# Moving the sums of the down-projection's weights into the first up-projection, the operand groups of x a step later, and the first pair's weights into other pages

## The chip, the cores and the metric

The kernel runs on one core of a Trainium2 chip. The metric is the device time of one execution in microseconds (us); several runs are made and their median is taken. The core's engines run side by side, each through its own list of instructions: TensorE (PE in the profile) multiplies matrices, VectorE (DVE) and ScalarE (ACT) work element by element, GpSimd (POOL) and SyncE (SP) do little here but issue transfers. Transfers between the main memory (HBM) and the on-chip memory (SBUF) are carried by 16 DMA engines that all issuers share. Matmul results stand in PSUM, from where DVE or ACT takes them.

## The reference, cut to what matters

One layer of a decoder on x of 2048 positions by 1024 channels:

```python
h = rms_norm(x, norm1_g)
lru_x, lru_gate, sc_b, sc_c, sc_x = jnp.split(h @ w_in, splits, axis=-1)   # 1024 -> 2*1024 + 3*512
lru_x = causal_dwconv(lru_x, lru_conv_w) + lru_conv_b                      # 4 taps
y_lru = rg_lru(lru_x, ...) * gelu(lru_gate)          # gates by 16 blocks of 64x64, then a scan along time
y_sc = sc_b * causal_dwconv(sc_c * sc_x, sc_conv_w)                        # 3 taps
x = x + concatenate([y_lru, y_sc]) @ w_out                                 # 1536 -> 1024
h = rms_norm(x, norm2_g)
gate, up = jnp.split(causal_dwconv(h @ w_up, ffn_conv_w), 2, axis=-1)      # 1024 -> 2*3072, 3 taps
x = x + (gelu(gate) * up) @ w_down                                         # 3072 -> 1024
return rms_norm(x, final_g)
```

All of it is float32. The four matrix products w_in, w_out, w_up and w_down are nearly all of the arithmetic.

## The kernel before, in words

**Float32 by three matmuls.** `split` (L228, L229) makes of each operand a high part (ACT, a copy to the rounded type) and a low part (DVE, a subtraction). Each product of a 128x128 block of weights with 512 positions is then three matmuls: high by high, high by low, low by high. So ACT and DVE have a split to do for each weight and each operand, and TensorE waits for both parts.

**Fewer products.** Most block products of two by two are made with seven products instead of eight (Strassen's scheme in Winograd's form). They need sums and differences of blocks: of the weights, called S1 to S4 beside the plain blocks W11, W12, W22, W21, and of the operands, called T1 to T4 beside B11, B21, B22. `TERMS` lists the seven products as pairs of such names. The sums of the weights of w_in are made on DVE in the first stage and kept in HBM (`si_d`). Those of w_down are made by transfers alone, in HBM (`sd_d`): `sums` (L941 and on) writes a list `pieces` of 24 pieces of 512 KB, six each for S1, S3, S2, S4. `sum_step` (L400 to L407) takes the next piece: it issues a copy of one block on SP (L404), and with a lag of two steps a transfer on Pool that adds the other block to a copy made earlier (L407, an accumulate). S2 adds the finished S1, and S4 the finished S2, so some accumulates read what others have written.

**The stages.** The sequence is worked in two halves of 1024 positions:

1. in-projection of half 0 (`in_phase`, 0 to 336 us), with direct products;
2. out-projection of half 0 (`sweeps`, 336 to 458 us): seven sweeps of three steps, each step with 24 matmuls for each of two k (L992). Beside it, `x1_beside` (after steps 2, 6, 11 and 16 of 21) makes the operands of half 1's in-projection: four groups, one for each call of `x1_prep`. A group is two loads, a handful of DVE sums and differences (L607 to L614) and four splits with the names hhB11x, hhB21x, hhT1x, htx and their low parts;
3. in-projection of half 1 (`in_blocks`, 458 to about 790 us): 14 pairs of output blocks, 84 matmuls each (L666). The first pair goes through `spread`, which for each of four k runs all seven products; the others go term by term. Beside the pairs run the convolutions, the gates (L369, L380) and the scans. `beside_blocks(j)` is called once for a pair: `mean0` loads and squares the first half's result for its norm (L1140, L1147), and two calls of `sum_step` follow;
4. out-projection of half 1 (from about 790 us);
5. up-projection of half 0 (`up_phase(0)`, 942 to 1378 us): 24 pairs of 84 matmuls. `up_weights` issues three loads of weights for the pair after the next (L629 to L631), makes S1 to S4 on DVE (L640) and splits them. `UpPair.open` clears the first two columns of two pages with Pool (L329), and `keep_halo` copies the last two columns with Pool (L336);
6. down-projection of half 0 (1378 to 1607 us), the first that reads `sd_d`; then the up- and down-projection of half 1.

**What sets the order.** On TensorE, SP and Pool instructions run as the program writes them. On ACT and DVE a scheduler sets the order by priorities; `high_priority` moves some forward. Each engine's list is worked strictly in turn, so an instruction that waits holds all behind it.

**Pages.** SBUF tiles come from named rings; a tile waits until its page's last reader is done. Raw weights of the sweeps and of `up_weights` are loaded into "wr" (6 pages, `raw_tile`), their split parts stand in pages that `wpage` and `vpage` take by turns from a ring of ten: two "w" and eight "v". `in_weights` (L807 and on, loads at L816) loads two weight blocks of the in-projection at a time into a "w" page; for the first four terms of the first pair (`V0`) the split parts go to "v" pages, for all others to "wr".

Of the kernel before, what the change touches and what calls it, by code (L numbers as in the profile page):

```python
# [28 lines left out]
NR = 6  # L29
LP = 0  # L30
LW = 400
LEAD = 3
HALVES = (slice(0, P // 2), slice(P // 2, P))
HW = 90
# [3 lines left out]
NI = NFF // 2  # L38
# [29 lines left out]
PAIR_OF = {o: (PAIRS.index(p), i) for p, ab in BLOCKS.items() for i, o in enumerate(ab)}  # L68

TERMS = [("W11", "B11"), ("S1", "T1"), ("S2", "T2"), ("S3", "T3"), ("W22", "T4"), ("S4", "B22"), ("W12", "B21")]  # L70
V0 = [w for w, _ in TERMS[:4]]
KEPT = ["W11", "W12", "W22"]
SPILLED = ["S3", "S1", "S2", "S4"]

# [14 lines left out]
def block_kernel(  # L89
# [37 lines left out]
    def blocks(name, ops, n):  # L127
        return {o: [dr.tile([P, 2, NB], F32, name=f"{name}_{o}_{k}") for k in range(n // 2)] for o in ops}
# [4 lines left out]
    sd_d = blocks("sd_d", S_OPS, NI)  # L133
    si_d = [dr.tile([P, 4, NB], F32, name=f"si_d{i}") for i in range(len(PAIRS))]
    x2_d = [[dr.tile([2, P, T], F32, name=f"x2_d{h}_{m}") for m in range(KC // 2)] for h in range(NH)]
# [5 lines left out]
    def page(name, tag, bufs):  # L141
        return sb.tile([P, 2, NB], F32, name=name, tag=tag, bufs=bufs)
# [10 lines left out]
    def wv_page(name, tag):  # L153
        return page(name, tag, NW if tag == "w" else NWV - NW)

    def tmp(name):
        return page(name, "tmp", 7)
# [4 lines left out]
    def raw_tile(name):  # L162
        return page(name, "wr", NR)
# [7 lines left out]
    def flat(t):  # L171
        return t.rearrange("p a b -> p (a b)")
# [54 lines left out]
    def split(hi, lo, src):  # L227
        nc.scalar.activation(r32(hi), src, AF.Copy)  # L228
        nc.vector.tensor_tensor(r32(lo), src, hi, ALU.subtract)  # L229
# [71 lines left out]
    def mean_split(acc, name):  # L301
        n = acc.shape[-1]
        hi = flat(tmp(f"rh_{name}"))[:, :n]
        lo = flat(tmp(f"rl_{name}"))[:, :n]
        with tc.high_priority(offset=HP):
            split(hi, lo, acc)
        return hi, lo
# [93 lines left out]
    def sum_step():  # L401
        if pieces:
            dst, src, add = pieces.pop(0)
            nc.sync.dma_start(dst, src)  # L404
            adds.append((dst, add))
        if len(adds) > 2 or adds and not pieces:
            nc.gpsimd.dma_start(*adds.pop(0), accum_op=ALU.add, max_dma_last_dim=2 * T)  # L407
# [186 lines left out]
    def x1_prep(k, rs, side=0):  # L594
        return operands(f"x_{k}", k, lambda kk: xT[kk, :, T:S], O_G1, rs, side)
# [30 lines left out]
    def up_weights(half, j):  # L626
        n = f"up{half}_{j}"
        ta, tb, tcd = (raw_tile(f"wr{k}_{n}") for k in "abc")
        nc.sync.dma_start(ta[:, 0, :], w_up[j, 0])  # L629
        nc.sync.dma_start(tcd, w_up[j, 2:4].rearrange("h p c -> p h c"))  # L630
        nc.sync.dma_start(tb[:, 0, :], w_up[j, 1])  # L631
        tick()

        def two(src, name):
            hi, lo = wpage(f"wh{name}_{n}"), wpage(f"wl{name}_{n}")
            split(hi, lo, src)
            return [(hi[:, i, :], lo[:, i, :]) for i in range(2)]

        def add(dst, a, b):
            nc.vector.tensor_tensor(dst, a, b, ALU.add)  # L640

        w11, w12, w22, w21 = ta[:, 0, :], tb[:, 0, :], tcd[:, 0, :], tcd[:, 1, :]
        s1, s2, s3, s4 = ta[:, 1, :], tb[:, 1, :], tcd[:, 1, :], ta[:, 1, :]
        add(s1, w22, w21)
        add(s2, s1, w11)
        add(s3, w11, w21)
        p11, p1 = two(ta, "a")
        p12, p2 = two(tb, "b")
        p22, p3 = two(tcd, "c")
        add(s4, s2, w12)  # L650
        d = wpage(f"whd_{n}")
        split(d[:, 0, :], d[:, 1, :], s4)
        return {"W11": p11, "W12": p12, "W22": p22, "S1": p1, "S2": p2, "S3": p3, "S4": (d[:, 0, :], d[:, 1, :])}
# [112 lines left out]
    def up_rest(half, j, ug, un):  # L766
        cg, cu = flat(tmp(f"cg{half}_{j}")), flat(tmp(f"cu{half}_{j}"))
        conv(cu, un, 3, O_FCW + 3 * (NFF + j))
        conv(cg, ug, 3, O_FCW + 3 * j)
        nc.scalar.activation(cg, cg, AF.Gelu_apprx_tanh)  # L770
        nc.vector.scalar_tensor_tensor(cu, cg, -1.0, cu, ALU.mult, ALU.mult)
        when = {NFF - 2: 3, NFF - 1: 6}.get(j, 1)
        if j % 2 == 0:
            combine_even(f_d[half], when, j // 2, cu, cg)
            even.append((cu, cg))
        else:
            a, c = even.pop()
            combine_odd(f_d[half], when, j // 2, a, cu, c, (cg[:, :NB], cg[:, NB:]))

    def up_phase(half, hs, between):  # L780
        wts = [up_weights(half, 0), up_weights(half, 1)]
        cur = UpPair(half, 0, hs, wts[0])
        for j in range(NFF):
            if j + 2 < NFF:
                wts.append(up_weights(half, j + 2))
            nxt = UpPair(half, j + 1, hs, wts[j + 1]) if j + 1 < NFF else None
            if j == 0:
                cur.spread()
                nxt.begin()
                nxt.sum1()  # L790
            elif nxt is None:
                cur.middle(cur.sum1)
                cur.second()
                cur.fourth()
                cur.end()
            else:
                cur.middle(cur.second)
                nxt.begin()
                cur.fourth()
                if j + 2 < NFF:  # L800
                    nxt.sum1()
                cur.end()
            up_rest(half, j, cur.ug, cur.un)
            cur = nxt
            between(j)

    def in_weights(ops):  # L807
        n = "_".join(f"{i}{op}" for i, op in ops)
        raw, m = wv_page(f"wr_in{n}", "w"), len(ops)
        for at, (i, op) in enumerate(ops):  # L810
            if op in KEPT:
                o, h = BLOCKS[PAIRS[i]][op[1] == "2"], slice(0, NB) if op[2] == "1" else slice(NB, T)
                src = w_in[o][:, h]
            else:
                src = si_d[i][:, SPILLED.index(op), :]
            nc.sync.dma_start(raw[:, at, :], src)  # L816
        out = []
        for at, (i, op) in enumerate(ops):
            home = vpage if i == 0 and op in V0 else raw_tile
            t = home(f"w{op}_in{i}")  # L820
            split(t[:, 0, :], t[:, 1, :], raw[:, at, :])
            out.append((t[:, 0, :], t[:, 1, :]))
        return out
# [142 lines left out]
    def sums(src, dst, n):  # L966
        for o, a, b in SUMS:
            for i2 in range(n // 2):
                t = flat(dst[o][i2])
                add = src[W_OPS.index(b), i2] if b in W_OPS else flat(dst[b][i2])  # L970
                pieces.append((t, src[W_OPS.index(a), i2], add))

    def sweeps(half, wsrc, fsrc, ni, name, residual, done, beside, tail=0, lead=0):
# [6 lines left out]
        for s, (wo, fo, on_x) in enumerate(SWEEPS):  # L980
# [20 lines left out]
            for i2 in range(ni // 2):  # L1001
# [5 lines left out]
                parts = []  # L1007
                with tc.high_priority(offset=LW if step < lead else HW):
                    for raw, n in zip(raws, "wf"):
# [32 lines left out]
    def acc_tile(name):  # L1042
        return flat(tmp(f"ss_{name}"))
# [29 lines left out]
    tick()  # L1073
    tick()
    store_queue[0] = nc.sync
    sums(w_down, sd_d, NI)


    def x1_beside(s):
        if s in (2, 6, 11, 16):  # L1080
            hx.append(x1_prep(len(hx), ss1[1]))

    def wsrc(w, sums):
# [19 lines left out]
    def res_alloc(key, n):  # L1103
# [9 lines left out]
        x_residual(0, res_alloc),  # L1113
        store_done(x2_d[0], None, "b0"),
        x1_beside,
    )

    rs2 = [[], []]
# [12 lines left out]
    hs = [[], []]  # L1131
    def squares_then_mean(src, name, out, first):
        acc = acc_tile(name)
        held = []

        def between(n):
            k = n - first
            if 0 <= k < KC:
                t = flat(tmp(f"sx_{name}_{k}"))
                nc.sync.dma_start(t, src(k))  # L1140
                held.append(t)
            if 1 <= k <= KC:
                t = held[k - 1]
                if k == 1:
                    nc.scalar.activation(acc, t, AF.Square)
                else:
                    nc.scalar.activation(t, t, AF.Square)  # L1147
                    nc.vector.tensor_tensor(acc, acc, t, ALU.add)
            if k == KC + 1:
                held.append(mean_split(acc, name))  # L1150
            if k == KC + 2:
                out.append(inv_rms(acc, name, held[-1]))

        return between
# [2 lines left out]

    def beside_blocks(j):
        mean0(j)
        sum_step()  # L1160
        sum_step()

    store_queue[0] = nc.gpsimd
    late_gates = in_blocks(hx, beside_blocks)
    store_queue[0] = nc.sync

# [10 lines left out]
    def out1_beside(s):  # L1177
# [14 lines left out]
        out1_beside,  # L1192
        lead=LEAD,
    )

    up_phase(0, hs[0], squares_then_mean(lambda k: x2_d[1][k // 2][k % 2], "b1", rs2[1], 2))

    ss3 = acc_tile("c0")

# [151 lines left out]
```

## Time and profile before

| what | value |
|---|---|
| median of the runs | 2310.24 us (2309.06 to 2311.68, 3 runs) |
| the profiled execution | 2310.52 us |
| its span in the trace | 2308.7 us, 1.8 less |
| mean granted clock of TensorE | 0.988 |
| data moved by DMA | 415 MB, 180 GB/s in the mean |

The span is what the profiler sees between first and last instruction; the time of the run holds a little more around it. In a page's rows a line is `line engine operation out<-in`, with the count behind an x. A row of a time line gives the start in us, the length in us, and in brackets the engine's idle time before it and what ended it. In the rows of waits stand the total, the number of times and the longest. The granted clock is 1.00 at full speed. "SPq" and "POOLq" are transfers issued by SP and Pool.

### The profile page before, as it was taken

The page shows a single profiled execution, that of the slowest core. Times are in us where ns is not written, and L with a number is a line of the kernel's source. Part 1 is how long each engine was busy: PE and PEld are TensorE (multiplying, and loading weights), DVE is VectorE, ACT ScalarE, POOL GpSimd, SP SyncE. Part 2 cuts the span into 40 slices and gives each one's busy share as a digit, 9 for nine tenths or more (in the row PEclk, how much of TensorE's full clock was granted, in tenths as well). Part 3 has the DMA queues.
Part 4 walks back from the last instruction along what each step waited for, and adds up shares of the span by engine and source line. Part 5 has one row for each costly group of instructions (what it writes and reads, how often), then busy time and mean ns, then how long its engine had stood idle before and what let it go on. Part 6 is the DMA issues. An engine that isn't in the chain of part 4 may idle for free.

```text
span 2308.7 us, 26404 instructions
## 1 busy us (share of the span) xinstructions
PE 2242.5 (97%) x9750; PEld 1825.3 (79%) x9750; DVE 1787.3 (77%) x2070; ACT 1214.7 (53%) x1403; POOL 179.0 (8%) x298
## 2 busy tenths in 40 slices
PE   9999999999889989999999999999999999999997
PEld 7787787777667768888888888888888888888886
DVE  8868878846667799789898877677888888876556
ACT  7648834457577844455555444444554444443343
POOL 0021110000111100001010100000000000100000
PEclk9999999999999989999999999999999999999999
DMA  7575367657777868243332347676223232359754
GB/s 276 162 222 173 120 244 257 235 173 206 203 215 211 257 214 298 96 144 123 119 107 99 110 160 286 204 246 208 87 96 110 96 110 96 110 187 328 252 197 157
DMA packets 157952, 415.00 MB, mean 180 GB/s; under 512 B 16640, under 2 KB 19328, under 8 KB 157248
## 3 DMA queue, kind: packets, MB, share of 16 engines
q1 hardware_dynamic: 136960, 356.96, 45.1%
q0 software_dynamic: 20720, 56.37, 9.2%
q8 instruction: 76, 1.25, 0.2%
q14 instruction: 52, 0.43, 0.1%
q10 hardware_dynamic: 144, 0.00, 0.0%
HBM read 311.55 MB, written 139.46 MB: 195 GB/s over the span
## 4 chain that ended last, share of the span: by engine, by line
PE 65%; issue 2%; ACT 2%; DVE 2%; DMA 1%; POOL 0%; SPq 0%; DVEq 0%; ACTq 0%; POOLq 0%
PE zx L666 22%; PE dx L992 11%; PE zc L666 11%; PE dy L992 8%; PE za L666 5%; PE ox L992 2%; PE oy L992 2%; PE zxin L666 1%; PE zS L666 1%; PE zW L666 1%; PE zcin L666 0%; DMA sx_b<-x_d 0%; DMA wr_in9S_9S<-si_d 0%; DMA sd_d_S<-in_w_down 0%; ACT r L380 0%
## 5 line engine op out<-in xcount | busy, mean ns | idle before, releaser
L229 DVE TENSOR_TENSOR fl_d<-wrf_d,fh_d 128x1024 fp32r<-128x1024 f32 x84 | 102.7, 1223 | 120.3 <-ACT fh_d L228 117.9
L228 ACT ACTIVATE fh_d<-wrf_d 128x1024 fp32r<-128x1024 f32 x84 | 88.9, 1059 | 201.9 <-PE dy L992 78.3
L992 PE MATMUL dx<-fh_d,wh_d 128*128 128x512 f32 x384 | 149.4, 389 | 0.0
L992 PE MATMUL dx<-fl_d,wh_d 128*128 128x512 f32 x384 | 149.4, 389 | 0.0
L992 PE MATMUL dx<-fh_d,wl_d 128*128 128x512 f32 x384 | 149.4, 389 | 0.0
L229 DVE TENSOR_TENSOR wla_up<-wra_up,wha_up 128x1024 fp32r<-128x1024 f32 x48 | 58.8, 1225 | 110.0 <-ACT wha_up L228 110.0
L284 PE MATMUL zin_b<-xh,wl_in 128*128 128x512 f32 x448 | 138.7, 391 | 2.6 <-DVE wl_in L229 2.6
L284 PE MATMUL zin_b<-xh,wh_in 128*128 128x512 f32 x448 | 139.7, 393 | 0.7 <-ACT xh L452 0.4
L284 PE MATMUL zin_b<-xl,wh_in 128*128 128x512 f32 x448 | 138.7, 390 | 0.1
L345 DVE SCALAR_TENSOR_TENSOR cg<-ug,prm,cg 128x1024 f32<-128x1024 f32 x96 | 122.9, 1280 | 8.2 <-ACT cg L341 7.3
L345 DVE SCALAR_TENSOR_TENSOR cu<-un,prm,cu 128x1024 f32<-128x1024 f32 x96 | 122.8, 1279 | 4.7 <-ACT cu L341 4.3
L666 PE MATMUL zc<-hhB,whd_up 128*128 128x512 f32 x368 | 120.8, 389 | 0.0
L666 PE MATMUL zx<-ht,whc_up 128*128 128x512 f32 x368 | 113.3, 389 | 0.0
L992 PE MATMUL dy<-fh_d,wh_d 128*128 128x512 f32 x288 | 112.0, 389 | 0.0
L992 PE MATMUL dy<-fl_d,wh_d 128*128 128x512 f32 x288 | 112.0, 389 | 0.0
L992 PE MATMUL dy<-fh_d,wl_d 128*128 128x512 f32 x288 | 112.0, 389 | 0.0
L677 ACT ACTIVATE ug<-zx 128x512 f32<-128x512 f32 x92 | 54.9, 596 | 103.0 <-PE zx L666 98.1
L229 DVE TENSOR_TENSOR wl_d<-wrw_d,wh_d 128x1024 fp32r<-128x1024 f32 x84 | 102.3, 1219 | 8.3 <-ACT wh_d L228 7.0
L284 PEld LDWEIGHTS zin_b<-xh,wh_in 128*128 128x128 f32 x448 | 83.7, 188 | 24.4 <-DVE yc L557 1.5
L284 PEld LDWEIGHTS zin_b<-xh,wl_in 128*128 128x128 f32 x448 | 84.5, 189 | 20.6 <-DVE wl_in L229 3.0
L228 ACT ACTIVATE fh_o<-wrf_o 128x1024 fp32r<-128x1024 f32 x42 | 44.5, 1059 | 106.5 <-PE ox L992 28.3
L284 PEld LDWEIGHTS zin_b<-xl,wh_in 128*128 128x128 f32 x448 | 84.4, 188 | 18.1 <-DVE xl L453 0.5
(549 smaller groups left out, 6406.1 us busy)
## 6 DMA issues: line engine op xcount, KB each, us to landing
wrc_up<-in_w_up SPq DMA_DIRECT2D x48, 512.0 KB, 4.7
f_d_T<-cg SPq DMA_DIRECT2D x96, 256.0 KB, 2.5
wrw_d<-sd_d_S SPq DMA_DIRECT2D x48, 512.0 KB, 4.9
wrf_d<-f_d_T SPq DMA_DIRECT2D x48, 512.0 KB, 4.1
f_d_B<-cu SPq DMA_DIRECT2D x72, 256.0 KB, 2.4
wrw_d<-in_w_down SPq DMA_DIRECT2D x36, 512.0 KB, 4.8
wrf_d<-f_d_B SPq DMA_DIRECT2D x36, 512.0 KB, 3.4
wr_in<-in_w_in SPq DMA_DIRECT2D x25, 512.0 KB, 7.1
```

Of the source, the lines that this page charges most:

```text
L228: nc.scalar.activation(r32(hi), src, AF.Copy)
L229: nc.vector.tensor_tensor(r32(lo), src, hi, ALU.subtract)
L284: nc.tensor.matmul(ps[t], r32(a), r32(b[:, blk(t)]), start=(first and i == 0), stop=(last and i == 2))
L345: nc.vector.scalar_tensor_tensor(dst, src[:, k : k + T], col(o_w + k), dst, ALU.mult, ALU.add)
L666: nc.tensor.matmul(ps, r32(p[:, s]), r32(self.hs[k][x][o]), start=f and i == 0, stop=l and i == 2, skip_group_check=True,)
L677: nc.scalar.activation(dst, self.x, AF.Copy)
L992: nc.tensor.matmul(ps[m], r32(p), r32(x[:, k, :]), start=first and i == 0 and n == 0, stop=(last or not on_x) and i == ni - 1 and n == 2, ...
```

## The change

Three edits, all of order and place; the arithmetic stays.

1. The list of the w_down sums is written just before `up_phase(0)` and no longer before the first sweeps, and the two calls of `sum_step` leave `beside_blocks`. A new `beside_pairs(j)` calls what ran beside the up-projection's pairs before (the loads, squares and norm of the second half's result) and from pair 2 on two `sum_step`s for each pair. With 24 pieces that is pairs 2 to 13, and the last accumulates a pair later.
2. `x1_beside` makes its first three groups a step later, after steps 3, 7 and 12; the fourth stays after 16.
3. `V0` holds all seven terms. In `in_weights`, a load whose first block belongs to the first pair lands in a "wr" page and not in a "w" page, and its parts go to "v" pages: the seven blocks of pair 0, and W11 of pair 1, which shares a load with the last of them.

```diff
+NS = 2
+J0 = 2
...
-V0 = [w for w, _ in TERMS[:4]]
+V0 = [w for w, _ in TERMS]
...
     def in_weights(ops):
         n = "_".join(f"{i}{op}" for i, op in ops)
-        raw, m = wv_page(f"wr_in{n}", "w"), len(ops)
+        early = ops[0][0] == 0 and ops[0][1] in V0
+        raw = raw_tile(f"wr_in{n}") if early else wv_page(f"wr_in{n}", "w")
...
-            home = vpage if i == 0 and op in V0 else raw_tile
+            home = vpage if early else raw_tile
...
-    sums(w_down, sd_d, NI)
...
     def x1_beside(s):
-        if s in (2, 6, 11, 16):
+        if s in (3, 7, 12, 16):
...
     def beside_blocks(j):
         mean0(j)
-        sum_step()
-        sum_step()
...
-    up_phase(0, hs[0], squares_then_mean(lambda k: x2_d[1][k // 2][k % 2], "b1", rs2[1], 2))
+    sums(w_down, sd_d, NI)
+    mean1 = squares_then_mean(lambda k: x2_d[1][k // 2][k % 2], "b1", rs2[1], 2)
+
+    def beside_pairs(j):
+        mean1(j)
+        for _ in range(NS if j >= J0 else 0):
+            sum_step()
+
+    up_phase(0, hs[0], beside_pairs)
```

What this does to the lists of the engines stands in their orders, shown at three places. First VectorE in the first out-projection, around the first group of x. The names with "_o_1_0" are step 0 of sweep 1; fl and wl are low parts of operand and weight, xr the sums that take TensorE's results; hax, hbx and hcx belong to the group. Before:

```order
L229 TENSOR_TENSOR fl_o_0_2_2767<-wrf_o_0_2_2760,fh_o_0_2_2766 128x1024
L607 SCALAR_TENSOR_TENSOR hax_2796<-hax_2796,g_71,ss_a_742 128x1024
L611 TENSOR_TENSOR hcx_2802<-hax_2796 128x512
L607 SCALAR_TENSOR_TENSOR hbx_2797<-hbx_2797,g_71,ss_a_742 128x1024
L612 SCALAR_TENSOR_TENSOR hcx_2802<-hcx_2802,hbx_2797 128x512
L613 TENSOR_TENSOR hax_2796<-hbx_2797,hax_2796 128x512
L229 TENSOR_TENSOR wl_o_1_0_2836<-wrw_o_1_0_2831,wh_o_1_0_2835 128x1024
L1029 TENSOR_TENSOR xr_11_0_2732<-xr_11_0_2732,ox_0_2680 128x512
L1029 TENSOR_TENSOR xr_11_0_2732<-xr_11_0_2732,ox_1_2681 128x512
L229 TENSOR_TENSOR fl_o_1_0_2840<-wrf_o_1_0_2833,fh_o_1_0_2839 128x1024
```

And now, at the same place:

```order
L231 TENSOR_TENSOR fl_o_0_2_2767<-wrf_o_0_2_2760,fh_o_0_2_2766 128x1024
L231 TENSOR_TENSOR wl_o_1_0_2809<-wrw_o_1_0_2804,wh_o_1_0_2808 128x1024
L231 TENSOR_TENSOR fl_o_1_0_2813<-wrf_o_1_0_2806,fh_o_1_0_2812 128x1024
L1032 TENSOR_TENSOR xr_11_0_2732<-xr_11_0_2732,ox_0_2680 128x512
L1032 TENSOR_TENSOR xr_11_0_2732<-xr_11_0_2732,ox_1_2681 128x512
L1032 TENSOR_TENSOR xr_11_1_2770<-xr_11_1_2770,ox_2_2682 128x512
L609 SCALAR_TENSOR_TENSOR hax_2844<-hax_2844,g_71,ss_a_742 128x1024
L1032 TENSOR_TENSOR xr_11_1_2770<-xr_11_1_2770,ox_3_2683 128x512
L609 SCALAR_TENSOR_TENSOR hbx_2845<-hbx_2845,g_71,ss_a_742 128x1024
L613 TENSOR_TENSOR hcx_2850<-hax_2844 128x512
L231 TENSOR_TENSOR wl_o_1_1_2876<-wrw_o_1_1_2871,wh_o_1_1_2875 128x1024
```

Both low parts of step 0 of sweep 1 stand ahead of the group; the group's first operations stand between them and the parts of step 1.

Second ScalarE in the in-projection of half 1, around the sigmoids of the second gate. The numbers behind wr_in are the pairs of the two blocks in that load; soin and xlin are copies of products out of PSUM. Before:

```order
L1147 ACTIVATE sx_b_2_4190<-sx_b_2_4190 128x1024
L677 ACTIVATE soin_4187<-zxin_4090 128x512
L228 ACTIVATE wS_in_4201<-wr_in4S_5W_4198 128x512
L380 ACT_TABLE_LOAD
L380 ACTIVATE r_1_4285<-zr_1_b_4277,prm 64x512
```

```order
L380 ACTIVATE i_1_4286<-zi_1_b_4280,prm 64x512
L677 ACTIVATE xlin_4234<-zxin_4236 128x512
L228 ACTIVATE wW_in_4204<-wr_in4S_5W_4198 128x512
L228 ACTIVATE wW_in_4210<-wr_in5W_4W_4207 128x512
```

Now:

```order
L1149 ACTIVATE sx_b_2_4180<-sx_b_2_4180 128x1024
L679 ACTIVATE xlin_4220<-zxin_4222 128x512
L230 ACTIVATE wS_in_4187<-wr_in4S_5W_4184 128x512
L230 ACTIVATE wW_in_4190<-wr_in4S_5W_4184 128x512
L679 ACTIVATE soin_4177<-zxin_4080 128x512
L230 ACTIVATE wW_in_4196<-wr_in5W_4W_4193 128x512
L382 ACT_TABLE_LOAD
L382 ACTIVATE r_1_4271<-zr_1_b_4263,prm 64x512
```

```order
L382 ACTIVATE i_1_4272<-zi_1_b_4266,prm 64x512
L679 ACTIVATE xlin_4220<-zxin_4222 128x512
L230 ACTIVATE wW_in_4199<-wr_in5W_4W_4193 128x512
```

Two more splits of weights stand ahead of the eight sigmoids; the copy xlin still stands behind them.

Third Pool in the up-projection of half 0, at the end of pair 3. u_halo takes the last columns of the pages un and ug; the memsets clear the first columns of pair 5's pages. Before:

```order
L336 COPY u_halo<-un_3_7260 128x2
L336 COPY u_halo<-ug_3_7258 128x2
L329 MEMSET ug_5_7544 128x2
L329 MEMSET un_5_7546 128x2
L336 COPY u_halo<-un_4_7400 128x2
```

Now:

```order
L338 COPY u_halo<-un_3_7212 128x2
L338 COPY u_halo<-ug_3_7210 128x2
L409 DMA sd_d_S_0_225<-in_w_down 256x512
L409 DMA sd_d_S_1_226<-in_w_down 256x512
L331 MEMSET ug_5_7502 128x2
L331 MEMSET un_5_7504 128x2
L338 COPY u_halo<-un_4_7354 128x2
```

Two accumulates stand ahead of the next memsets. On SP the two copies of a pair (L404, now L406) leave the places behind the loads of `mean0` and stand ahead of the next three loads of up weights. TensorE's order is the same in both kernels.

## The prediction

> **What bounds the kernel now.** I read the head of the page first, to see which engine is full.
>
> ```profile
> span 2308.7 us, 26404 instructions
> ...
> PE 2242.5 (97%) x9750; PEld 1825.3 (79%) x9750; DVE 1787.3 (77%) x2070; ACT 1214.7 (53%) x1403; POOL 179.0 (8%) x298
> ```
>
> TensorE is busy for 97% of the span, so no edit that leaves its 9750 matmuls alone can gain more than the time in which it stands or runs below its full pace. The second view, the busy time by stage, says where that time is. Columns: stretch; its length; busy time and count of PE, PEld, DVE, ACT, POOL; granted clock; DMA share; GB/s.
>
> ```profile
> 336.00:458.00 122.00, 116.51 (x510) 95.14 (x509) 105.03 (x120) 53.13 (x56) 1.45 (x2) 1.00 0.71 257
> 458.00:484.00 26.00, 22.36 (x84) 16.30 (x83) 9.04 (x15) 6.56 (x11) 3.29 (x4) 0.87 0.73 222
> ...
> 556.00:640.00 84.00, 69.05 (x277) 52.88 (x275) 58.41 (x73) 56.89 (x77) 13.15 (x20) 0.94 0.72 207
> 640.00:710.00 70.00, 58.90 (x231) 43.38 (x232) 46.00 (x56) 54.11 (x71) 9.44 (x13) 0.93 0.75 204
> ...
> 800.00:840.00 40.00, 28.85 (x105) 22.30 (x104) 35.86 (x41) 17.02 (x19) 5.41 (x10) 0.83 0.84 298
> ...
> 942.00:1378.00 436.00, 436.00 (x1925) 361.04 (x1924) 371.66 (x420) 226.42 (x268) 45.27 (x92) 1.00 0.36 119
> ```
>
> The last row is the first up-projection: never idle, clock 1.00, so 436.0/1925 = 0.2265 us is the pace of one matmul. What a stretch loses is its length less its matmuls at that pace: 6.5 us in 336–458 (**A**, the first out-projection's sweeps), 7.0 in 458–484 (**B**, the first pair of the second half's in-projection), 21.3 and 17.7 in 556–640 and 640–710 (**C**, its later pairs, 39.0 in all), 16.2 in 800–840 (**D**, the start of the second out-projection), and nothing in the up-projection. The DMA engines stand the other way: 0.71 to 0.84 busy where TensorE loses, 0.36 where the sums go.
>
> The third view, PE's waits within A and then within 484–710, names the releasers (total, times, longest).
>
> ```profile
> PE oy L992 <- DVE fl_o L229: 2.8, 2, 2.3
> PE ox L992 <- DVE fl_o L229: 2.7, 2, 2.0
> ```
>
> ```profile
> PE zr_b L369 <- DVE cv L345: 6.1, 2, 4.4
> PE zxin L666 <- ACT xlin L677: 5.6, 2, 3.7
> PE zxin L666 <- DVE wW_in L229: 5.5, 2, 3.5
> PE zxin L666 <- ACT soin L677: 4.9, 2, 4.6
> PE zxin L666 <- ACT wW_in L228: 2.7, 2, 1.5
> PE zxin L666 <- ACT prin L677: 0.9, 1, 0.9
> PE zxin L666 <- ACT wS_in L228: 0.3, 1, 0.3
> ```
>
> The waits of C sum to 26.0 us, but the stretch loses 39.0. The other 13.0 is the clock (0.94 and 0.93 there): a wait costs about 39.0/26.0 = 1.5 times itself. Even a short one does it, as a row from the first stage shows:
>
> ```profile
> 100.00:120.00 20.00, 17.39 (x71) 13.97 (x70) 19.51 (x27) 6.29 (x6) 4.06 (x6) 0.91 1.07 380
> ```
>
> There 2.6 us idle (20.00 less 17.39) came with a clock of 0.91, and 71 matmuls at pace are 16.1 us, so 3.9 us were lost. The Trainium skill ("TensorE: Matmul & The Clock Gate", section "What's actually happening") has the clock halve after an idle window of about 3.4 us. Taken strictly, only C's waits above that would be multiplied, and the gain of C below would be some 17 us by my estimate and not 21; the row decides for the factor.
>
> **A: the x groups a step later.** The first group's DVE operations stand ahead of the next steps' splits. Rows of DVE:
>
> ```profile
> 345.81 1.28 DVE L607 SCALAR_TENSOR_TENSOR hax<-hax,g,ss_a 128x1024 f32<-128x1024 f32 x1
> ...
> 352.59 1.22 DVE L229 TENSOR_TENSOR fl_o<-wrf_o,fh_o 128x1024 fp32r<-128x1024 f32 x1
> ...
> 355.52 1.22 DVE L229 TENSOR_TENSOR hlB11x<-hax,hhB11x 128x1024 fp32r<-128x1024 f32 x1
> ...
> 360.67 1.22 DVE L229 TENSOR_TENSOR fl_o<-wrf_o,fh_o 128x1024 fp32r<-128x1024 f32 x1
> ```
>
> Four group operations from 345.81 on put off the split that ends near 353.8, and the hl splits from 355.52 on the one that ends near 361.9; these are two of A's four waits (5.5 us in all). In the new order both operands of the next step are split ahead of the group. The group does not shrink; it goes behind, and what is late next is the split of the step after it. Counted along the new order at the durations above, I expect two of the four waits to go and the other two to add up to some 4 us with the clock: −2.5 us. Bounds: −4 (one wait left) and +1 (the lump only moves). The two loads of each group move with it, behind one more step's loads on SP; nothing on SP waits for them.
>
> **B: the first pair's weights in other pages.** Now the raw weights go to the two pages "w", which the last sweep's matmuls hold. SP issues them only as these come free, and ACT's splits wait for them:
>
> ```profile
> 457.62 0.80 SPq L816 DMA_DIRECT2D wr_in0S_0S<-si_d  x2
> ...
> 462.82 0.88 SPq L816 DMA_DIRECT2D wr_in0W_1W<-in_w_in  x2
> ```
>
> ```profile
> 460.52 0.63 ACT L228 ACTIVATE wS_in<-wr_in0S_0S 128x512 fp32r<-128x512 f32 x1 [3.88 <-DMA wr_in0S_0S<-si_d]
> ...
> 466.50 0.63 ACT L228 ACTIVATE wS_in<-wr_in0W_0S 128x512 fp32r<-128x512 f32 x1 [1.43 <-DMA wr_in0W_0S<-si_d]
> ```
>
> ```profile
> 448.07 1.22 DVE L229 TENSOR_TENSOR fl_o<-wrf_o,fh_o 128x1024 fp32r<-128x1024 f32 x1
> ```
>
> TensorE is at the first pair from 458 on. The pages "wr" are read by splits alone, and this DVE row, the sweep's last, ends at 449.3: raw blocks in these pages can be on their way eight us before the "w" pages let them. The hi and lo parts need eight pages "v"; those hold operands of the last three steps and come free step by step, in the order in which the products are due. The seven splits (0.63 us each on ACT) then run ahead of the seven products (three matmuls each, 0.68 us): −7.0 us, the whole loss. Bounds: −7.0, and −2 if the last pages of the sweep, free only at 458, hold back the later products. Pair 1 follows with 63 more matmuls of pair 0 as cover (14.3 us), so I cost its later loads at nothing; without that cover it would be the same few us again.
>
> **C: the sums leave the in-projection.** 24 copies on SP and 24 accumulates on Pool, 512 KB each, go. The price they take shows in the landing of a weight (median us to landing), first in a quiet moment, then between sums:
>
> ```profile
> wr_in3W_4S<-si_d SPq DMA_DIRECT2D x1, 256.0 KB, 3.0
> ...
> wr_in4S_5W<-si_d SPq DMA_DIRECT2D x1, 256.0 KB, 11.1
> ```
>
> ACT works in its order, so a late weight also holds what stands behind it:
>
> ```profile
> 552.05 0.63 ACT L228 ACTIVATE wS_in<-wr_in4S_5W 128x512 fp32r<-128x512 f32 x1 [4.96 <-DMA wr_in4S_5W<-si_d]
> ...
> 559.60 0.60 ACT L677 ACTIVATE xlin<-zxin 128x512 f32<-128x512 f32 x1
> ```
>
> ACT stood 4.96 us for that block, then ran its eight sigmoids, and the copy xlin, which TensorE awaited, came at 559.60. So I let the waits on weights (5.5 + 2.7 + 0.3) and on xlin (5.6) go: 14.1 us, times 1.5, −21 us. The waits on cv, soin and prin (11.9 us, 18 with the clock) are chains of DVE and ACT without a transfer, and stay. Bounds: −8 (only the one row of 5.5 goes, times 1.5) and −41 (everything, with 2 us after 710). Against the upper end: in 556–710 ACT is busy 111.0 us and the matmuls at pace are 115, so two engines that hand work to and fro have almost no slack. The new order also splits weights earlier on ACT, ahead of sigmoids; where one lands late, it holds them.
>
> **D.** Loads and operations there keep their order: 0, between −3 (stores on Pool no longer behind accumulates) and +2.
>
> **The sums in the up-projection.** One pair is 84 matmuls, 19.03 us. It gets two copies and two accumulates. Their price, by share of the 16 DMA engines: in a stretch of 5.8 us with one accumulate (first row), and in one of 7.1 us with two copies and two weight blocks (second).
>
> ```profile
> q0 software_dynamic: 272, 0.52, 60.2%
> ```
>
> ```profile
> q1 hardware_dynamic: 662, 2.13, 86.1%
> ```
>
> An accumulate is 0.602 × 5.8 = 3.5 us of all engines, a copy of 0.5 MB about 1.4 (6.1 us for 2.13 MB). Per pair 2 × 3.5 + 2 × 1.4 = 9.8; with the 0.36 × 19.03 = 6.9 there now, 16.7 of 19.03 us: 0.88 busy, in 12 or 13 of the 24 pairs. It fits, and what hides it is the lead of the weights and the slack of Pool:
>
> ```profile
> 994.22 0.44 SPq L629 DMA_DIRECT2D wra_up<-in_w_up  x1
> ```
>
> ```profile
> 1012.86 0.68 DVE L640 TENSOR_TENSOR wra_up<-wrc_up 128x512 f32<-128x512 f32 x1
> ```
>
> ```profile
> 756.49 0.90 POOL L407 DMA_DIRECT2D sd_d_S<-sd_d_S  x1 [4.96 <-issue]
> ```
>
> ```profile
> POOL u_halo L336 <- DVE ug L681: 203.2, 22, 10.5
> ```
>
> A weight is issued 18.6 us before DVE first adds it; even landing in 11.1 us instead of some 5 it leaves 7 us. The copies stand on SP ahead of the next pair's weights and cost only their issue, about 1 us for two. On Pool the second accumulate waits some 5 us until the first has landed, and behind it stand the memsets and halo copies of the coming pairs; but these wait now, up to 10.5 us, for DVE. DVE is busy 371.66 of 436 us, so a late weight could be made good only slowly. I take +1.5 us for a few late splits: bounds 0 (no wait in 436 us now, so no gain to be had) and +5. Without the cover see rival 3. The Trainium skill ("DMA: Bandwidth & Descriptors", section "Issuing engines are not separate DMA queues") speaks against the change: whichever engine issues them, all transfers share the same 16 DMA engines, so moving the sums removes none of their cost. The trace agrees (3.0 against 11.1 us above); it is the emptier stage that makes the difference.
>
> **Sum.** −2.5 − 7.0 − 21 + 0 + 1.5 = −29. The profiled execution took 2310.5 us (span 2308.7), 0.3 above the median of the runs: about 2281 us.
>
> **Rivals.**
> 1. The in-projection is bound by ACT and DVE, and C stays: −2.5 − 7.0 + 1.5 = −8, 2302 us. For: ACT's 111.0 us beside 115 of TensorE. Against: waits of ACT with a DMA as releaser, like the 4.96 us.
> 2. All of C goes: −2.5 − 7.0 − 41 + 1.5 = −49, 2261 us. For: every wait of C lies near a late transfer. Against: cv, soin and prin are released by engines.
> 3. Slower: the DMA engines fill up in the first up-projection. If accumulates and copies cost 1.5 times as much beside the weights (14.7 us a pair) and the base is 0.40 of a pair (7.6) while squares are loaded, a pair takes 22.3 us for 19.03, weights come later with each pair, and over 12 pairs +39 falls in, against −30.5 for the rest: 2319 us. It decides once the four sums of a pair take over 11.4 us of all engines. Against: 9.8 us by the rows, and the shares of 0.84 to 1.07 that the trace shows were reached by transfers of the same kinds. By the skill's rule above, this is where the moved cost would come back.
> 4. The change does nothing that counts: the pages "v" are as late as "w" were, the lump of A moves, and C goes only as far as the up-projection loses: about 2308 us.
>
> **How the numbers follow.** Forecast 0.64, its own range 2270 to 2297 (C from −8 to −32, B from −2, the up-projection up to +5). Rival 1: 0.16; rival 2: 0.07; rival 3: 0.06; rival 4: 0.07. The range of eight in ten reaches from between the forecast and rival 2 over rival 1: 2264 to 2304. A measurement of this kernel tells 0.2%, or 4.6 us. Faster by more: forecast, rivals 1 and 2, less 0.01 for their edges, 0.86; within it: rival 4 and that edge, 0.08; slower: rival 3, 0.06.
>
> **What would show it.** Right: in the stretch from 458 the first pair at clock 1.00 with no ACT wait on a raw block; in the in-projection a DMA share near 0.5, weights landing in 3 to 5 us, a loss near 18 us there; in the up-projection a DMA share near 0.9 in pairs 2 to 14 with TensorE still at 0.2265 us a matmul. Wrong: PE waits on up weights, or DVE waits on wrc_up (rival 3); waits on cv and xlin as long as now with weights landing early (rival 1).

## The result, and the profile after

The changed kernel takes 2275.98 us (median of 4 runs, 2275.51 to 2277.45) against 2309.93 us before (4 runs, 2309.06 to 2311.68): a ratio of 0.9853, with a 95% interval of 0.9836 to 0.9870. That is 34 us less; the forecast was 2281, the range 2264 to 2304. The profiled execution took 2275.72 us, its span is 2273.9 us. TensorE's busy time and count, from the page after:

```profile
span 2273.9 us, 26402 instructions
...
PE 2228.6 (98%) x9750; PEld 1819.8 (80%) x9750; DVE 1788.1 (79%) x2070; ACT 1214.4 (53%) x1403; POOL 173.8 (8%) x298
```

The busy times of DVE and ACT are those of before within a microsecond, so no work went. What went is waiting, and 13.9 us of TensorE's busy time at the same 9750 matmuls, with its mean granted clock up from 0.988 to 0.993. Where it went is seen from the times of TensorE's first matmul of each stage. The table gives the stages' lengths in us in the two profiled executions.

| stage | before | after | difference | forecast |
|---|---|---|---|---|
| first in-projection | 336.7 | 334.9 | −1.8 | 0 |
| A: first out-projection | 121.0 | 119.9 | −1.1 | −2.5 |
| B: first pair | 26.4 | 19.0 | −7.4 | −7.0 |
| C: later pairs | 305.4 | 279.5 | −25.9 | −21 |
| D: second out-projection | 130.9 | 132.3 | +1.3 | 0 |
| first up-projection | 457.9 | 457.9 | 0.0 | +1.5 |
| all that follows | 930.4 | 930.4 | 0.0 | 0 |

The busy time by stage after, in stretches that follow the stages' new times (A, B, C, the start of D, the up-projection):

```profile
335.00:455.00 120.00, 116.53 (x506) 95.64 (x505) 108.13 (x125) 55.84 (x62) 1.45 (x2) 0.99 0.77 277
455.00:474.00 19.00, 19.00 (x85) 15.76 (x84) 8.53 (x14) 5.85 (x9) 1.44 (x2) 1.00 0.60 194
474.00:753.00 279.00, 268.29 (x1159) 210.51 (x1159) 200.67 (x244) 215.20 (x285) 17.24 (x32) 0.99 0.41 134
753.00:790.00 37.00, 25.04 (x100) 19.38 (x98) 29.09 (x32) 19.73 (x22) 5.40 (x10) 0.85 0.76 277
...
908.00:1344.00 436.00, 436.00 (x1925) 361.02 (x1925) 371.90 (x419) 226.45 (x267) 62.33 (x116) 1.00 0.61 177
```

The first pair is never idle and at full clock. In C the DMA share is 0.41, and 279.0 − 1159 × 0.2265 = 16.5 us are lost. The up-projection has the same 1925 matmuls in 436 us as before, while its DMA share went from 0.36 to 0.61. TensorE's waits after, in A and then in C:

```profile
PE ox L995 <- DVE fl_o L231: 2.6, 1, 2.6
PE oy L995 <- DVE fl_o L231: 0.9, 1, 0.9
```

```profile
PE zr_b L371 <- DVE cv L347: 8.1, 3, 5.7
PE zxin L668 <- ACT xlin L679: 1.3, 2, 0.9
PE zxin L668 <- ACT soin L679: 0.9, 1, 0.9
PE zxin L668 <- DVE wW_in L231: 0.4, 1, 0.4
```

In C mainly the waits on cv are left; those on weights, on xlin and on soin are nearly gone.

### The profile page after: what moved, and what is told of

It is laid out like the page before. It is cut to its first block, busy times and chain, and to the rows that moved or that the text cites. A ratio compares the mean times of both kernels' runs of the same rounds, so it can differ in the third digit from the quotient of the medians.

```text
span 2273.9 us, 26402 instructions
## 1 busy us (share of the span) xinstructions
PE 2228.6 (98%) x9750; PEld 1819.8 (80%) x9750; DVE 1788.1 (79%) x2070; ACT 1214.4 (53%) x1403; POOL 173.8 (8%) x298
## 4 chain that ended last, share of the span: by engine, by line
PE 86%; DVE 5%; ACT 4%; issue 3%; DMA 1%; POOL 0%; DVEq 0%; SPq 0%; ACTq 0%; POOLq 0%
PE zx L668 22%; PE dx L995 11%; PE zc L668 11%; PE zin_b L286 10%; PE dy L995 9%; PE za L668 6%; PE ox L995 5%; PE oy L995 4%; PE zxin L668 3%; PE zcin L668 1%; PE zS L668 1%; PE zain L668 1%; PE zr_b L371 1%; PE zW L668 1%; DVE r L395 1%
```

## The experiments

Lengths are of one profiled execution each, in us, in the stages of the table above. Each ratio is to runs of the kernel before that were made beside that run (their medians lie from 2310.2 to 2312.0). A stage that an edit doesn't touch differs between executions, too: the first in-projection by 3.8 us (334.8 to 338.6), D by 4.2 (129.0 to 133.2), A by 1.6 (118.4 to 120.0 with the new order), C by 1.1 (279.5 to 280.6 in the four runs with its new order and no added transfer). The change's own parts first.

| run | median, ratio to before (95%) | A | B | C | D | up |
|---|---|---|---|---|---|---|
| before | 2309.9 | 121.0 | 26.4 | 305.4 | 130.9 | 457.9 |
| after | 2276.0, 0.9853 (0.9836 to 0.9870) | 119.9 | 19.0 | 279.5 | 132.3 | 457.9 |
| sums only | 2285.7, 0.9898 (0.9883 to 0.9914) | 121.0 | 26.6 | 280.6 | 132.5 | 457.9 |
| x groups only | 2308.6, 0.9992 (0.9984 to 1.0001) | 119.9 | 27.3 | 305.7 | 131.6 | 457.9 |
| pages only | 2303.3, 0.9969 (0.9957 to 0.9981) | 121.6 | 19.0 | 306.4 | 129.0 | 457.9 |
| copies early | 2292.1, 0.9919 (0.9906 to 0.9932) | 119.9 | 19.0 | 293.1 | 132.0 | 459.2 |
| copies on Pool | 2298.4, 0.9940 (0.9925 to 0.9955) | 118.4 | 19.0 | 297.5 | 133.2 | 458.6 |
| small sums | 2291.8, 0.9912 (0.9892 to 0.9932) | 119.9 | 19.0 | 294.5 | 131.1 | 460.2 |
| small sums on Pool | 2279.4, 0.9866 (0.9849 to 0.9882) | 119.9 | 19.0 | 282.1 | 132.8 | 458.7 |
| extra accumulates | 2286.1, 0.9888 (0.9874 to 0.9903) | 118.4 | 19.5 | 290.5 | 131.5 | 457.9 |
| three a pair | 2306.4, 0.9978 (0.9968 to 0.9987) | 120.0 | 19.0 | 280.0 | 131.9 | 491.5 |
| four a pair | 2331.7, 1.0086 (1.0070 to 1.0102) | 118.4 | 19.0 | 280.4 | 131.6 | 515.3 |
| L7 earlier | 2284.5, 0.9885 (0.9869 to 0.9900) | 119.9 | 19.0 | 290.2 | 129.2 | 459.3 |
| splits first | 2280.5, 0.9866 (0.9850 to 0.9881) | 119.9 | 19.0 | 281.4 | 130.9 | 458.3 |

### Each edit alone

Sums only is the changed kernel with

```diff
-V0 = [w for w, _ in TERMS]
+V0 = [w for w, _ in TERMS[:4]]
-        if s in (3, 7, 12, 16):
+        if s in (2, 6, 11, 16):
```

and the loads of `in_weights` in "w" pages as before. 

> Only the sums move (edit 1); the x groups and the first pair's pages stay as before. Theory 1 (the sums' data make the weights of the in-projection land late, and each edit acts in its own stage): the pairs after the first take 280 us and not 305, the first pair stays at 26.4, the first out-projection at 121, the up-projection at 457.9; time about 2284.5 us, that is -25. Theory 2 (part of the gain in the later pairs comes from the first pair's earlier pages, which start the whole in-projection on time): the later pairs stay at 290 or more, time 2295 or more.

X groups only is the kernel before with the steps (3, 7, 12, 16). 

> Only the x groups begin a step later (edit 2). Theory 1: the first out-projection takes 119.9 us for 121.0, nothing else moves: about 2309, that is -1, not to be told from no change. Theory 2 (the groups' place also sets when the first pair's weights are split, so that edit 2 matters for the first pair): the first pair gets shorter than 25 us, time 2307 or less.

Pages only is the kernel before with the third edit's lines. 

> Only the first pair's raw weights land in the other pages (edit 3); the sums stay in the in-projection. Theory 1: the first pair takes 19.0 us for 26.4, the later pairs stay at 305: about 2302.5, that is -7.4. Theory 2 (the earlier start is lost again, since the later pairs wait for weights that are slowed by the sums and not for the first pair): later pairs 309 to 313, time 2306 to 2310.

All three did what the first theory said: C 280.6, A 119.9, B 19.0, and the other stages where they were. The differences of the medians (−24.6, −1.6, −7.0) add up to −33.2, the whole change gives −34.0, so no dependence of the edits on each other shows. The x groups alone can't be told from no change in the time. In that run two more lines show B's cause, TensorE's wait on a split and ScalarE's wait for its raw block, which the pages edit removes:

```profile
PE zW22in L666 <- ACT wW_in L228: 3.4, 1, 3.4
```

```profile
466.82 0.63 ACT L228 ACTIVATE wW_in<-wr_in0W_0S 128x512 fp32r<-128x512 f32 x1 [4.03 <-DMA wr_in0W_0S<-in_w_in]
```

### Copies or accumulates, data or place

The next runs ask what in the sums cost the 26 us. First the copies alone were put back into the in-projection:

```diff
     def beside_blocks(j):
         mean0(j)
+        copy_step()
+        copy_step()
...
-            sum_step()
+            add_step()
```

> The changed kernel, but the 24 copies on SP stay in the in-projection, two a pair, and only the 24 accumulates on Pool go to the up-projection. Theory 1 (share of the 16 DMA engines decides; a copy takes 1.4 us of all engines, an accumulate 3.5): some three tenths of the 26 us come back, later pairs about 287 us, time about 2284. Theory 2 (the place of the copies on SP ahead of the weights' loads decides): nearly all comes back, later pairs 300 or more, time 2297 or more. Theory 3 (accumulates alone are the cause): 280, time 2276.

C took 293.1 us, half of the 26 back: more than the share of the copies (the first theory) and less than all. Something was missing in all three theories. In this run ScalarE's order in C is that of before (by the names in the traces, all rows that stand elsewhere lie ahead of 490 us); in the changed kernel it isn't. So the next run added sums almost without data, 16 KB each, two a pair:

```diff
+    spare = [dr.tile([4, T], F32, name=f"spare_{i}") for i in range(24)]
...
+            nc.sync.dma_start(dst, src)
...
+            nc.gpsimd.dma_start(*small_adds.pop(0), accum_op=ALU.add, max_dma_last_dim=2 * T)
```

> The changed kernel with added work: in the in-projection 24 copies on SP and 24 accumulates on Pool stand at the places of before, but of 16 KB each and into memory that nothing reads. Nearly all issues of before, a thirty-second of the data; ScalarE's order comes out nearly as before (15 of 1404 rows differ). Theory 1 (data): later pairs about 280 us, time about 2276. Theory 2 (issues and order): later pairs 293 or more, time 2289 or more; all of it would be 305 and 2301.

With a thirty-second of the data C still took 294.5 us: the first theory, mine, fell for half of the gain. ScalarE's order in C is that of before in this run, too. Time line of ScalarE in this run, then SP's row for the load of the weights that it splits last, and its median time to landing:

```profile
562.24 0.60 ACT L679 ACTIVATE prin<-zxin 128x512 f32<-128x512 f32 x1 [0.27 <-PE zxin L668]
568.63 1.24 ACT L345 ACTIVATE cv<-xlin,prm 128x1024 f32<-128x1024 f32 x1 [5.79 <-DVE xlin L683]
569.78 1.04 ACT L1149 ACTIVATE sx_b<-sx_b 128x1024 f32<-128x1024 f32 x1
570.73 0.57 ACT L679 ACTIVATE soin<-zxin 128x512 f32<-128x512 f32 x1
571.20 1.14 ACT L230 ACTIVATE wW_in<-wr_in6W_6W 128x512 fp32r<-128x512 f32 x2
```

```profile
553.50 0.81 SPq L819 DMA_DIRECT2D wr_in6W_6W<-in_w_in  x2
```

```profile
wr_in6W_6W<-in_w_in SPq DMA_DIRECT2D x2, 256.0 KB, 5.0
```

The weights were there at about 559. ScalarE stood idle from 562.8 to 568.6, since the convolution's first step, which waits for DVE, stands ahead of their split; then sx_b and soin stand ahead too, and on DVE three more operations. TensorE waited (this run, C):

```profile
PE zxin L668 <- DVE wW_in L231: 5.5, 2, 3.5
PE zxin L668 <- ACT soin L679: 2.9, 2, 2.2
PE zxin L668 <- ACT wW_in L230: 2.4, 2, 1.5
```

These are, to the tenth, the 5.5 us and nearly the 2.7 us on wW_in of before. The kernel before, at the same place, has the same picture (ScalarE, SP, then the time to landing):

```profile
583.43 1.25 ACT L343 ACTIVATE cv<-xlin,prm 128x1024 f32<-128x1024 f32 x1 [5.78 <-DVE xlin L681]
...
586.00 1.14 ACT L228 ACTIVATE wW_in<-wr_in6W_6W 128x512 fp32r<-128x512 f32 x2
```

```profile
568.30 0.95 SPq L816 DMA_DIRECT2D wr_in6W_6W<-in_w_in  x2
```

```profile
wr_in6W_6W<-in_w_in SPq DMA_DIRECT2D x2, 256.0 KB, 7.3
```

There the blocks had landed by about 576, ten us before their split. The control has the same small transfers with the copies issued by Pool (`nc.gpsimd` for `nc.sync`), which leaves both orders in C as in the changed kernel, row for row:

> The run with the small sums again (24 copies and 24 accumulates of 16 KB added in the in-projection), but the small copies are issued by Pool and not by SP. The transfers are the same; what differs is that ScalarE's and VectorE's orders now come out as in the changed kernel, row for row (0 rows differ), where with the copies on SP they came out nearly as before. Theory 1 (the order cost the 15 us of that run): later pairs 279 to 282 us, time 2275 to 2279. Theory 2 (the added transfers or issues cost them, whatever the order): later pairs 290 us or more, time 2286 or more.

C took 282.1 us and the run 2279.4, a little past the bounds of the first theory (282 and 2279). The order is worth 294.5 − 282.1 = 12.3 us (before rounding), the small transfers and their issues 2.6. Of the 12.3 us, 4.8 are TensorE's waits (17.6 against 12.8 us) and the rest its clock, 0.91 against 1.00 from 560 to 640. A rival would be the copies' issues on SP, which only the first of the two runs has. But in C ScalarE stood only 6.2 us for blocks of weights in that run, and 10.1 us in the changed kernel, so those issues made no weights late. ScalarE in the control, at the same place:

```profile
566.07 1.24 ACT L345 ACTIVATE cv<-xlin,prm 128x1024 f32<-128x1024 f32 x1 [5.04 <-DVE xlin L683]
567.21 0.62 ACT L230 ACTIVATE wW_in<-wr_in6W_6W 128x512 fp32r<-128x512 f32 x1
567.74 1.05 ACT L1149 ACTIVATE sx_b<-sx_b 128x1024 f32<-128x1024 f32 x1
```

The wait for DVE is there as well, but the first split follows it at once, and TensorE's wait on DVE's wW_in is 0.4 us in all of C.

The other half is data. Extra accumulates puts 24 full accumulates (without copies) into the in-projection of the changed kernel, with that kernel's own order of ScalarE but for one row:

```diff
+            nc.gpsimd.dma_start(*more.pop(0), accum_op=ALU.add, max_dma_last_dim=2 * T)
```

> The changed kernel with added work: 24 accumulates of 512 KB on Pool in the in-projection, two a pair, into memory that nothing reads (four copies in the first stage fill it), and none of the copies on SP there; ScalarE's order as in the changed kernel (1 row differs). Theory 1 (data): the 13 us that the copies left over come back, later pairs 292 to 297 us, time 2288 to 2293. Theory 2 (order): later pairs 280 to 284, time below 2281.

C took 290.5 us, 11.0 more: under the 292 that the first theory had as its least, well over the second. ScalarE here stands for late weights (these blocks landed after 6.6 us, in the changed kernel after 3.0), and what TensorE awaits stands behind (ScalarE's rows, then TensorE's waits in C):

```profile
578.98 0.63 ACT L230 ACTIVATE wS_in<-wr_in5S_6S 128x512 fp32r<-128x512 f32 x1 [4.26 <-DMA wr_in5S_6S<-si_d]
581.27 0.63 ACT L230 ACTIVATE wS_in<-wr_in5S_6S 128x512 fp32r<-128x512 f32 x1 [1.67 <-DMA wr_in5S_6S<-si_d]
...
594.61 0.60 ACT L679 ACTIVATE xlin<-zxin 128x512 f32<-128x512 f32 x1
```

```profile
PE zxin L668 <- ACT xlin L679: 10.6, 2, 5.4
```

This is the mechanism of the forecast, at the operation that it named. Last, the full copies of the first of these runs, issued by Pool:

```diff
-            nc.sync.dma_start(dst, src)
+            nc.gpsimd.dma_start(dst, src)
```

> As the run with the copies early, but the 24 copies of the in-projection are issued by Pool and not by SP; ScalarE's and VectorE's orders come out as in the changed kernel. Theory 1 (the data of the copies slow the weights, whoever issues them): later pairs about 293 us as in that run, time about 2291. Theory 2 (a copy on SP, or the order of ScalarE that the scheduler makes of it, is what costs): later pairs 283 or less, time 2281 or less.

C took 297.5 us, beyond what either theory gave: 15.4 us more than with the small sums on Pool, in the same order, while on SP full copies cost no more than small ones (293.1 against 294.5). Those two stand in the order of before, whose own waits may hide late data; copies on SP in the new order were not run. Issues and landings of this run, around one urgent weight, wr_in5S_6S (Pool, SP, then KB each and median us to landing):

```profile
571.23 1.95 POOL L1164 DMA_DIRECT2D sd_d_S<-in_w_down  x4
```

```profile
574.04 1.01 SPq L819 DMA_DIRECT2D wr_in5S_6S<-si_d  x2
```

```profile
q0 software_dynamic: 427, 2.99, 100.1%
q1 hardware_dynamic: 29, 0.06, 4.4%
...
wr_in5S_6S<-si_d SPq DMA_DIRECT2D x2, 256.0 KB, 10.3
```

Pool had stood behind its own stores and issued four copies at once, just ahead of the weight: Pool's queue took all of the DMA engines, SP's 4%, and the weight landed after 10.3 us. On SP two copies went out just behind the same weight, which landed after 3.0 us:

```profile
wr_in5S_6S<-si_d SPq DMA_DIRECT2D x2, 256.0 KB, 3.0
```

ScalarE stood 8.7 us for the block in the first case. So at this place a transfer's price was set by which load it went ahead of, and not by its share alone; the other places were not compared.

### How much the up-projection can take

> The changed kernel with four sums a pair in the first up-projection and not two, so in six pairs and not twelve. By the shares, 4 x 3.5 + 4 x 1.4 + 7.6 = 27.2 us of all DMA engines for a pair of 19.03. Theory 1 (full DMA engines hold the weights back, the third rival's mechanism): 6 pairs, some 5 to 8 us each less the 7 us of lead, 25 to 40 us, time 2300 to 2315. Theory 2 (Pool issues one accumulate per 5.85 us, so the surplus queues on Pool, the weights still land within 18 us of their issue and TensorE doesn't notice): up-projection 458 to 461 us, time 2276 to 2279.

> The changed kernel with three sums a pair in the first up-projection, so eight pairs. The run with four a pair lost 57 us there, with ScalarE waiting for Pool. Theory 1 (Pool's line: an accumulate is issued only when the one before has landed, 5.85 us each; four are 23.4 us and overrun a pair of 19.03, three are 17.6 and just fit): up-projection 458 to 464 us, time 2276 to 2282. Theory 2 (the 16 DMA engines are full: 3 x 4.9 + 7.0 = 21.7 us of all engines a pair, over 19.03): 2.7 us and more in each of eight pairs, up-projection 475 us or more, time 2292 or more.

Only `NS` differs, 4 and 3 for 2. The up-projection took 515.3 and 491.5 us for 457.9: 57.4 and 33.6 us lost. With four that is beyond the 25 to 40 of the first theory, with three it is the second theory's loss. My third rival's arithmetic gives 6 × (4 × 4.9 + 7.6 − 19.03) = 49 and 8 × (3 × 4.9 + 7.6 − 19.03) = 26 us, so its threshold of 11.4 us of sums a pair lies where the runs put it, between 9.8, which cost next to nothing, and 14.7, which cost much; nothing between was run. Pool's line at 5.85 us each (17.6 us fit) did not foresee the loss at three. But the wait isn't on weights. With three a pair, ScalarE's waits between 960 and 1200, and Pool's time line:

```profile
ACT ug L679 <- POOL u_halo L338: 57.2, 6, 18.8
```

```profile
1036.95 0.89 POOL L409 DMA_DIRECT2D sd_d_S<-in_w_down  x1 [12.25 <-DMA wrc_up<-in_w_up]
1049.85 0.90 POOL L409 DMA_DIRECT2D sd_d_S<-in_w_down  x1 [12.00 <-issue]
...
1050.48 0.53 POOL L338 COPY u_halo<-un 128x2 f32<-128x2 f32 x1
```

With the DMA engines near full (0.93 from 1000 to 1040), the accumulates on Pool follow each other after 8 to 13 us and not after 5.85. Pool issues the next one only when the one before has landed, whatever releaser the row names: in the trace these land at 1036.64 and 1049.53, 0.3 us ahead of the next issue. The halo copy stands behind them, ScalarE's copy ug needs the page that the halo copy reads, and TensorE needs ScalarE's copy. DVE waited 10.5 us for wrc_up there, TensorE 24.0 us for ug. With two a pair, five stretches of 38 us show shares of 0.80, 0.87, 0.85, 0.83 and 0.79, and this is one:

```profile
998.00:1036.00 38.00, 38.00 (x169) 31.45 (x169) 33.82 (x39) 20.52 (x25) 5.78 (x12) 1.00 0.87 237
```

### Two attempts at what is left

L7 earlier: `PAIRS` with `L6 L7 X2 X3` for `L6 X2 L7 X3`, against the 16 us lost at D's start.

> The changed kernel with the pair L7 before X2 and not after it, so that the last gate and scan no longer fall into the start of the second out-projection. Theory 1 (the 16 us lost at that start are the chain of the last gate, scan and products on ScalarE and VectorE): second out-projection 122 to 127 us for 132.3, time 2266 to 2271. Theory 2 (the start waits for the first loads and splits of the sweep whatever the last pair is): 131 or more, time 2275 or more.

D was 3.1 us shorter, between the two theories and no more than D differs where nothing is touched, but C rose by 10.7: 2284.5 us, slower than the changed kernel. The wait in D moved (7.5 us on fh_o at once), and in C TensorE's waits on cv add up to 11.8 us for 8.1, the last of them 4.5 us for 0.5. Splits first raises the priority of the splits:

```diff
+            with tc.high_priority(offset=200):
                 split(t[:, 0, :], t[:, 1, :], raw[:, at, :])
```

> The changed kernel with only the scheduler's priority of the weights' splits in the in-projection raised, no transfer added, moved or taken away: 34 of 1404 rows of ScalarE and 42 of VectorE stand elsewhere. If the order of ScalarE and VectorE alone makes differences of several us in the later pairs (theory 1: it made half of the gain there), these pairs move by 3 us or more from 279.5, to either side. If only transfers count (theory 2), they stay within 278 to 281 and the time within 2274.5 to 2277.5.

C took 281.4 us, between what the two theories allow, and the time of 2280.5 us is above the second's, so the run decides nothing. Inside it a wait did move: the longest one on cv is 8.6 us for 5.7. No run beats the changed kernel.

## Why the prediction was right, point by point

- **The bound.** TensorE loses only to waits and their clock, stage by stage: right. The up-projection took the sums for nothing in the profiled execution (0.0 for +1.5; 457.9 to 460.2 in the runs that kept two sums, or accumulates alone, a pair), with a share of 0.79 to 0.87 where 0.88 was worked out.
- **B.** −7.4 for −7.0, alone and together. The last raw block of the first pair goes out at 441.89 for 462.82 before. The prediction counted with eight us of lead; here it is some 20. No wait of TensorE is left in the stretch 455 to 474.
- **A.** The step was mis-sized: −1.1 for −2.5. Two of four waits went, as counted, but the other two are 0.9 and 2.6 us, and the second brings a low clock of its own (0.83 from 370 to 380). In every run with the new order A is shorter than in the three with the old one (118.4 to 120.0 against 121.0 to 121.6), but in the time alone the edit isn't measurable.
- **C.** −25.9 for −21: sign and size hold, one step failed. "So I let the waits on weights (5.5 + 2.7 + 0.3) … go" was right in that they went, wrong in why: those on wW_in, 8.2 of the 8.5 us, came from the order of ScalarE and DVE, not from late landings, as the run with small sums shows. At the factor of 1.5 that is 12.3 of the 21 us, and they came in by luck: its sum had no term for the order, and moving the sums happened to change it. My views of before held the sign of it: ScalarE's idle time ahead of cv was released by DVE, with the split of weights that had long landed right behind (the rows at 583.43 and 586.00 above). The wait on xlin was late data, as said. Of 25.9 us, 12.3 are order and 11.0 accumulates, if the two add up as measured apart; the 2.6 left are about the small run's issues, and whether they are that or scatter between executions stays open. The rest of 16.5 us against "18 stay": cv stayed (8.1 us in all of C for 6.9 before), soin did not (0.9 for 5.6).
- **D and the first stage.** +1.3 and −1.8 lie within what these stages differ by where nothing is touched. In the first stage the wait is the same (below); in D TensorE's waits have the same releasers and add up to 12.7 us for 11.2. Neither is claimed for the change.
- **The rivals.** The first (C bound by engines) was half right in what it blamed and wrong in the outcome: the engines' work did not bind, its order did. The third has its threshold where it said, between two and three sums a pair, with Pool's line as the place and not the weights. Its sign was there in small with two: VectorE waited 6.4 us for wrc_up, in eight waits, for 0.2 before, and TensorE did not notice.

## What to carry to other kernels

A transfer that moves can change more than the load on the DMA engines: here two issues a pair less on SP came with other lists for ScalarE and VectorE from the scheduler, and that was half of the gain in C (why the scheduler moves them is not shown). Before a wait is put down to a late transfer, look whether the data had landed and what stood ahead on the engine; a dummy transfer of a few KB at the same place separates order from data. Here the work moved to an emptier stage was free up to a point that the shares foretold, and past it the first to break was what stood behind that work in Pool's list.

## What the runs showed of the hardware

The accumulates on Pool go one at a time. In the traces of before, after, three and four a pair none of the 24 accumulates was issued earlier than 0.31 us after the one before it had landed, though each writes a piece of its own, while four copies on Pool went out within 1.95 us. Whether the chip or the program makes them wait is not shown.

The same wait cost different time in two executions. In 100 to 120 us, in code that no edit touches, TensorE waited 2.6 us for the same split in both kernels; before, 71 matmuls were done at a clock of 0.91, after, this row:

```profile
100.00:120.00 20.00, 17.41 (x77) 14.12 (x76) 19.37 (x27) 6.37 (x6) 4.07 (x6) 1.00 1.06 381
```

77 matmuls at 1.00, so 6 × 0.2265 = 1.4 us came from the clock alone. The Trainium skill ("TensorE: Matmul & The Clock Gate", section "What's actually happening") says that the window by which the clock is set runs free of the kernel; the two rows agree, since a wait of one length came with a low clock once and not the other time. The factor of 1.5 for a wait is thus a mean and not a price of each.
